# The order of the seven products of a weight pair, and where the seventh operand of the feed-forward is made

## The chip, the cores and the metric

One core of a Trainium2 chip runs the whole kernel. The metric is the device time of one execution in microseconds, as the median of several runs. The engines work side by side and are tied by semaphores: TensorE (PE) multiplies, VectorE (DVE) combines two tensors, ScalarE (ACT) copies, casts and applies functions, GpSimd (POOL) issues accumulating DMAs here, and SyncE (SP) issues all other DMAs.

## What is computed

One layer of a bidirectional encoder on 1024 positions of 1024 channels, in float32. The two parts that the change touches are dense projections: the combined input projection of the token mixers, and the gated feed-forward.

```
proj = h @ W_in                          # h: 1024 x 1024, W_in: 1024 x 8192
...
x  = x + y @ W_out
h2 = rmsnorm(x)
gate, val = split(h2 @ W_up)             # W_up: 1024 x 5632, D_FF = 2816
x  = x + (silu(dwconv3(gate)) * val) @ W_down
return rmsnorm(x)
```

## The kernel before

Activations lie transposed, with 128 channels on the partitions and 512 positions (a half) in a page of 128 x 512. Each float32 operand is split into a high part in a rounded format (fp32r) and the remainder as a low part (`split`, L120: ScalarE casts the high part, VectorE subtracts for the low part), and a product of two blocks is three matmuls, high-high, high-low and low-high (`mm3`, L138 to L145).

**Pairs.** 34 of the 64 column blocks of the input projection (17 pairs) and all 44 of the feed-forward's up projection (22 pairs: a gate block and the value block that belongs to it) are worked in pairs by a Strassen-like scheme of seven products instead of eight (`pair_job`, L223). A pair is a 2 x 2 matrix of quadrants (two halves of positions, two column blocks) over an inner dimension cut into two times four blocks of 128. A product is 4 blocks x 3 matmuls = 12 matmuls. Seven operands come from the activations, `acts(i)`, as differences and sums of the four quadrants b11, b12, b21, b22; seven from the weights, `w[i]`.

`prep` (L231 to L254) makes the weight operands: two raw tiles are loaded by SP (`raw_w` into tag `wr`; `sw`), a third (`w4`, the quadrant a22); GpSimd adds by accumulating DMAs (L237), and after each sum a cast and a subtraction split the result. Pages of tag `wp` hold operands 1 and 2, then 6 and 3 (4 buffers, in the main pool); pages of tag `wq` hold 7 and 5 together and 4 (3 buffers, in the pool `wpool`). The single `sw` tile is free for the next pair when 7 and 5 have been split.

`run` (L256 to L282) issues the products to TensorE in the order 1, 2, 6, 7, 5, 4, 3. Products 1, 6, 5 and 3 accumulate in one PSUM bank, `row` (tag `mm`, 3 buffers), 2 has a bank of its own (`tr`), 7 and 4 share `col` (`sc`). ScalarE copies a running sum out of a bank (`copy`, L265: p1 after 1, u2 after 6, p7 after 7), and VectorE makes the quadrants from such a copy and a bank (`evac`). TensorE's order is the order in which the program writes the matmuls, by hand; the other engines' orders and the DMA queues come from a planner that takes instructions as they become ready in its own estimate, the earlier written first. A write to a bank waits for the reads of it that were written before.

`run_jobs` (L149) prepares the weights of the next pair after four pieces (products 1 and 2) of the present one.

**The feed-forward's operands.** While the output projection `w_out` runs, each new page of normalised input (`x2`, scaled but without the row's norm factor) is stored to DRAM (`d_h2`) and kept in the pool `p4`. The loop at L1111 makes operands 1, 2, 6 and 5 from these tiles into 32 pages `hx` in the main pool. Then `p4` is released and the pool `fu` is laid over the same memory; a tile there waits until the tiles that lay under it are no longer used. Operands 7, 4 and 3 are made after the first products of the feed-forward have been issued, from reloads of `d_h2` (`late_load`, L1189; `late_parts`, L1186): eight loads for 7, four for 4, four for 3, through 4 pages `ft`.

**The gate.** `ffn_job` (L1131): quadrants with e = 0 are the gate columns, written to a padded row `gp` and scaled (L1142, L1144); quadrants with e = 1 are the values (L1138). When the second half of the gate has come, for both halves ScalarE and VectorE do the three taps (L1150, L1154), Silu (L1162), the norm factor (L1163), the product with the value (L1164) and the store to `d_g` (L1165). After the feed-forward the down projection reloads `d_g` in groups (`load_g`, L1220), and its first pass copies banks to `xr` (L1230).

Of the kernel before, what the change touches and what calls it, by code (L numbers as in the profile page):

```python
# [10 lines left out]
F32 = mybir.dt.float32  # L11
F32R = mybir.dt.float32r
# [3 lines left out]
ALU = mybir.AluOpType  # L16
AX = mybir.AxisListType

P = 128
# [25 lines left out]
def tile_hybrid_encoder(  # L45
# [22 lines left out]
    nc = tc.nc  # L68
    PSUM = bass.MemoryType.PSUM
    V, A, G, T = nc.vector, nc.scalar, nc.gpsimd, nc.tensor  # L70
# [20 lines left out]
    def nm(s):  # L91
        uid[0] += 1
        return f"{s}_{uid[0]}"
# [3 lines left out]
    def bank(tag):  # L97
        return ps.tile([P, H], F32, tag=tag, name=nm(tag), bufs=BANKS[tag])

    def page(pool, tag, bufs, dt=F32):  # L100
        return pool.tile([P, H], dt, tag=tag, name=nm(tag), bufs=bufs)

    def tmp():
        return page(mp, "tm", 4)
# [4 lines left out]
    def hx():  # L109
        return page(mp, "hx", 32, F32R)  # L110
# [6 lines left out]
    def split_lo(eng, lo, src, hi):  # L117
        eng.tensor_tensor(lo, src, hi.bitcast(F32), op=ALU.subtract)  # L118

    def split(hi, lo, src, eng):  # L120
        A.copy(hi, src)  # L121
        split_lo(eng, lo, src, hi)
        return hi, lo
# [4 lines left out]
    def raw_w(src, nk):  # L128
        t = mp.tile([P, nk, P], F32, tag="wr", name=nm("wr"), bufs=2)
        nc.sync.dma_start(t, src)  # L130
        return t

    def w_page(nk, pool=None):
        if pool is None:
            return mp.tile([P, nk, P], F32R, tag="wp", name=nm("wp"), bufs=4)
        return pool.tile([P, nk, P], F32R, tag="wq", name=nm("wq"), bufs=3)

    def mm3(acc, w, act, k, first, last, again=False):  # L138


        whi, wlo = w
        ahi, alo = act
        T.matmul(acc, whi[:, k, :], ahi, start=first, stop=False, skip_group_check=again)  # L143
        T.matmul(acc, whi[:, k, :], alo, start=False, stop=False, skip_group_check=again)  # L144
        T.matmul(acc, wlo[:, k, :], ahi, start=False, stop=last, skip_group_check=again)  # L145
# [77 lines left out]
    def pair_job(src0, src1, nk, acts, wpool, pool, evac, su=4):  # L223

        def prep():  # L231
            def both(src, alt):
                hi, lo = split(w_page(2 * nk, alt), w_page(2 * nk, alt), src, V)
                return [(hi[:, :nk], lo[:, :nk]), (hi[:, nk:], lo[:, nk:])]

            def add(o, a):
                G.dma_start(o, a, accum_op=ALU.add)  # L237

            w = {}
            rows = raw_w(src0, 2 * nk)  # L240
            col = wpool.tile([P, 2 * nk, P], F32, tag="sw", name=nm("sw"), bufs=1)
            nc.sync.dma_start(col[:, :nk], src0[:, :nk])
            nc.sync.dma_start(col[:, nk:], src1[:, :nk])
            a22 = wpool.tile([P, nk, P], F32, tag="w4", name=nm("w4"), bufs=1)
            nc.sync.dma_start(a22, src1[:, nk:])
            add(col, src1)
            w[1], w[2] = both(rows, None)
            add(rows[:, :nk], col[:, nk:])
            w[7], w[5] = both(col, wpool)
            add(rows[:, nk:], rows[:, :nk])  # L250
            w[6], w[3] = both(rows, None)
            one = w_page(2 * nk, wpool)
            w[4] = split(one[:, :nk], one[:, nk:], a22, V)
            return w  # L254

        def run(w):  # L256
            def product(i, acc, first=True):
                for k in range(nk):
                    mm3(acc, w[i], acts(i)[k], k, first and k == 0, k == nk - 1, not first)
                    if k % 2 == 1 or k == nk - 1:  # L260
                        yield

            def copy(acc):
                t = page(pool, "su", su)
                A.copy(t, acc)  # L265
                return t

            row, b2, col = bank("mm"), bank("tr"), bank("sc")
            yield from product(1, row)
            p1 = copy(row)  # L270
            yield from product(2, b2)
            evac(0, 0, b2, p1, ALU.add)
            yield from product(6, row, False)
            u2 = copy(row)
            yield from product(7, col)
            p7 = copy(col)
            yield from product(5, row, False)
            evac(1, 1, p7, row, ALU.subtract)
            yield from product(4, col, False)
            evac(1, 0, col, u2, ALU.subtract)  # L280
            yield from product(3, row, False)
            evac(0, 1, row)  # L282

        return prep, run

# [88 lines left out]
    def scratch(name, *dims):  # L374
        if not dims:
            return dp.tile([P, H], F32, name=name)
        return [scratch(f"{name}_{i}", *dims[1:]) for i in range(dims[0])]
# [14 lines left out]
    d_g = scratch("d_g", NF, 2)  # L392
# [5 lines left out]
    NK2 = ND // 2  # L398
# [128 lines left out]
    for k in range(NK2):  # L527
        b21 = page(p1, "su", 4)
# [133 lines left out]
    for half in range(2):  # L662
        xs = []
        for j in range(NCW):
            if j % 2 == 0:
                both = p1.tile([P, 2, H], F32, tag="ca", name=nm("cx"), bufs=2)
# [16 lines left out]
        for j, xn in enumerate(xs):  # L683
# [3 lines left out]
            both = gp0.tile([P, 2, H], F32R, tag="gl", name=nm("ch"), bufs=NCW)  # L687
# [313 lines left out]
    for h in range(NH):  # L1001
# [4 lines left out]
        for half in range(2):  # L1006
            i = 2 * h + half
# [33 lines left out]
    fw = tc.alloc_tile_pool(name="fw", bufs=1, reuse_waits="tile")  # L1041
# [30 lines left out]
    h2 = {i: [] for i in range(1, 8)}  # L1072
# [23 lines left out]
        return evac  # L1096

    h2_pages = {i: [(hx(), hx()) for _ in range(NK2)] for i in (1, 2, 6, 5)}

    def parts(i, k, src):  # L1100
        h2[i].append(split(*h2_pages[i][k], src, V))
# [9 lines left out]
    for k in range(NK2):  # L1111
        s_out.fill(16 if k else 17) if k < NK2 - 1 else s_out.drain()
        b11, b12, b21, b22 = x2[k][0], x2[k][1], x2[k + NK2][0], x2[k + NK2][1]
        t5, t6 = tmp(), tmp()
        parts(1, k, b11)
        V.tensor_tensor(t5, b11, b12, op=ALU.subtract)
        parts(2, k, b21)
        V.scalar_tensor_tensor(t6, t5, -1.0, b22, op0=ALU.mult, op1=ALU.subtract)
        parts(6, k, t6)
        parts(5, k, t5)  # L1120
    p4.release()


    fu = tc.alloc_tile_pool(name="fu", bufs=1, reuse_waits="tile")
# [5 lines left out]

    def ffn_job(j):  # L1131
        g = gp[j % 2]
        val = [None, None]

        def evac(e, half, x0, x1=None, op=None):
            if e == 1:
                val[half] = page(fu, "ft", 4)
                V.tensor_tensor(val[half], x0, x1, op=op)  # L1138
                return
            gh = g[:, 1 + half * H : 1 + (half + 1) * H]  # L1140
            if x1 is not None:
                V.tensor_tensor(gh, x0, x1, op=op)  # L1142
                x0 = gh
            V.tensor_tensor(gh, x0, rstd2[half], op=ALU.mult)  # L1144
            if half == 0:
                return
            for hf in range(2):
                o = hf * H
                c = tmp()
                A.activation(  # L1150
                    c, g[:, o : o + H], AF.Identity, scale=vec("fdw", j), bias=vec("fdb", j)
                )
                for k in (1, 2):
                    V.scalar_tensor_tensor(  # L1154
                        c,
                        g[:, o + k : o + k + H],
                        vec("fdw", k * NF + j),
                        c,
                        op0=ALU.mult,
                        op1=ALU.add,  # L1160
                    )
                A.activation(c, c, AF.Silu)  # L1162
                V.tensor_tensor(c, c, rstd2[hf], op=ALU.mult)  # L1163
                V.tensor_tensor(val[hf], val[hf], c, op=ALU.mult)  # L1164
                nc.sync.dma_start(d_g[j][hf], val[hf])  # L1165

        return pair_job(
            w_cols(ffn_w_up, 0, ND, j * P),
            w_cols(ffn_w_up, 0, ND, DFF + j * P),
            NK2,  # L1170
            lambda i: h2[i],
            fw,
            fu,
            evac,
            su=3,
        )
# [7 lines left out]
    rstd2 = [next(st) for st in stats]  # L1184

    def late_parts(i, src):  # L1186
        h2[i].append(split(page(fu, "hy", 24, F32R), page(fu, "hy", 24, F32R), src, V))

    def late_load(kk, half):  # L1189
        t = page(fu, "ft", 4)  # L1190
        nc.sync.dma_start(t, d_h2[kk][half])
        return t

    for k in range(NK2):
        b12, b22 = late_load(k, 1), late_load(k + NK2, 1)
        V.tensor_tensor(b12, b12, b22, op=ALU.subtract)
        late_parts(7, b12)
    for k in range(NK2):
        b21 = late_load(k + NK2, 0)
        for part in h2[6][k]:  # L1200
            V.tensor_tensor(b21, b21, part.bitcast(F32), op=ALU.add)
        late_parts(4, b21)
    for k in range(NK2):
        late_parts(3, late_load(k + NK2, 1))
    s_ffn.drain()
    fu.release()
    fw.release()
# [149 lines left out]
```

## Time and profile before

| | us |
|---|---|
| median of 3 runs | 1918.57 |
| lowest and highest | 1916.76 and 1922.56 |
| the profiled execution | 1916.23 |
| its span, first to last instruction | 1914.5 |
| mean granted TensorE clock | 0.974 |

How to read the profile: the page gives for each engine its busy time; a row of the view by stretch gives for a window, in microseconds from the span's start, the busy time and number of instructions of each engine (PE, PEld for the loading of weights, DVE, ACT, POOL), then the granted clock of TensorE, the share of the DMA engines and their rate. A row in order of time reads: start, duration, engine, line, operation, out<-in by names, shapes, count, and in brackets the idle time of the engine just before and what ended it. The shown duration of a matmul is longer than the distance to the next one, since they are pipelined; the distance between two starts is what counts. DMA rows (SPq, and L237 on POOL) show the issue, not the transfer. A row of the list of waits has: who waited for whom, microseconds in total, times, longest. A row of the DMA issues ends with the size and the median microseconds from issue to landing.

### The profile page before, as it was taken

To read this page: it belongs to the slowest core of one execution; us is meant where nothing else is said; L and a number is where in the kernel's file an instruction comes from. 1 tells how busy PE (TensorE), PEld (TensorE's weight loads), DVE (VectorE), ACT (ScalarE), POOL (GpSimd) and SP (SyncE) were. 2 spreads that over 40 slices of the span, in tenths; PEclk is the share of its full clock that TensorE was granted. 3 is DMA by queue.
4 is the path that set the end of the run, shared out by engine and by line. 5 is a ranking of instruction groups with operands and counts; after the bars stand their busy time and mean duration, and the time that the engine had idled before them with its cause. 6 is when DMAs were issued, how large, how long until landed. Compare 5 with 4: busy or idle time off the path is not lost.

```text
span 1914.5 us, 23761 instructions
## 1 busy us (share of the span) xinstructions
PE 1805.9 (94%) x8543; PEld 1484.6 (78%) x8543; DVE 1271.6 (66%) x1860; ACT 799.3 (42%) x1488; POOL 217.9 (11%) x218
## 2 busy tenths in 40 slices
PE   6989999999989999998997999899999999999996
PEld 4767888877778787887875888588888888788885
DVE  3488999535479898898845655766666666634445
ACT  6334343334555565455343134544443444522124
POOL 3101112213000101101000000111111111000000
PEclk8999999999999999999997999899999999999998
DMA  7747788885652332332227666767767775733134
GB/s 254 218 123 166 177 197 194 198 176 133 212 173 83 107 125 93 112 111 73 71 89 232 202 189 184 193 148 160 148 149 148 151 152 124 220 93 98 54 90 160
DMA packets 324492, 286.14 MB, mean 149 GB/s; under 512 B 14990, under 2 KB 245142, under 8 KB 324374
## 3 DMA queue, kind: packets, MB, share of 16 engines
q1 hardware_dynamic: 272582, 243.72, 41.1%
q0 software_dynamic: 51792, 40.90, 15.2%
q8 instruction: 67, 1.10, 0.2%
q14 instruction: 51, 0.42, 0.1%
HBM read 191.76 MB, written 72.35 MB: 138 GB/s over the span
## 4 chain that ended last, share of the span: by engine, by line
PE 60%; DVE 15%; DMA 11%; ACT 6%; issue 4%; POOL 2%; SPq 0%; ACTq 0%; POOLq 0%; DVEq 0%
PE mm L143 15%; PE mm L144 15%; PE mm L145 15%; PE sc L144 3%; PE sc L145 3%; PE sc L143 3%; DVE wp L118 2%; DVE acc L644 2%; DMA sw<-in_ffn_w_up_dram 2%; DMA sw<-in_w_in_dram 1%; DMA wr<-wr 1%; PE tr L145 1%; PE tr L143 1%; PE tr L144 1%; DVE DE L729 1%
## 5 line engine op out<-in xcount | busy, mean ns | idle before, releaser
L143 PE MATMUL mm<-hx,wp 128*128 128x512 f32 x1176 | 482.2, 410 | 21.6 <-ACT hx L121 6.3
L145 PE MATMUL mm<-hx,wp 128*128 128x512 f32 x1176 | 467.8, 398 | 3.7 <-DVE wp L118 3.7
L144 PE MATMUL mm<-hx,wp 128*128 128x512 f32 x1176 | 467.1, 397 | 3.3 <-POOL hx L118 1.9
L121 ACT CAST wp<-wr 128x1024 fp32r<-128x1024 f32 (+2 forms) x196 | 179.8, 918 | 337.2 <-PE mm L144 207.8
L118 DVE TENSOR_TENSOR wp<-wr,wp 128x1024 fp32r<-128x1024 f32 (+2 forms) x196 | 207.1, 1057 | 116.9 <-ACT wp L121 110.5
L143 PEld LDWEIGHTS mm<-hx,wp 128*128 128x128 f32 x1176 | 226.1, 192 | 72.0 <-ACT hx L121 8.5
L145 PEld LDWEIGHTS mm<-hx,wp 128*128 128x128 f32 x1176 | 225.2, 191 | 55.6 <-DVE wp L118 6.3
L144 PEld LDWEIGHTS mm<-hx,wp 128*128 128x128 f32 x1176 | 226.1, 192 | 49.9 <-POOL hx L118 3.5
L644 DVE SCALAR_TENSOR_TENSOR acc<-gl,v_b,acc 128x1024 f32<-128x1024 f32 x120 | 149.2, 1278 | 0.5
L143 PE MATMUL sc<-hy,wq 128*128 128x512 f32 x244 | 97.1, 398 | 2.8 <-ACT hy L121 2.8
L144 PE MATMUL sc<-hy,wq 128*128 128x512 f32 x244 | 96.7, 396 | 2.9 <-DVE hy L118 2.9
L145 PE MATMUL sc<-hy,wq 128*128 128x512 f32 x244 | 96.3, 395 | 0.0
L237 POOL DMA_DIRECT2D wr<-sw x39 | 34.9, 896 | 510.5 <-DVE wp L118 272.8
L1236 DVE TENSOR_TENSOR xr<-mm,xr 128x512 f32<-128x512 f32 x48 | 33.1, 690 | 81.5 <-PE mm L145 81.5
L837 PEld LDWEIGHTS sc<-qF,A 128*128 128x128 f32 x512 | 65.9, 193 | 19.2 <-ACT A L834 8.0
L837 PE MATMUL sc<-qF,A 128*128 128x128 f32 x512 | 69.2, 279 | 11.7 <-DVE qF L729 6.1
L121 ACT CAST wq<-sw 128x1024 fp32r<-128x1024 f32 x39 | 41.1, 1053 | 85.3 <-PE mm L144 66.6
L143 PE MATMUL mm<-hy,wp 128*128 128x512 f32 x156 | 63.2, 405 | 8.5 <-ACT wp L121 5.8
L1154 DVE SCALAR_TENSOR_TENSOR tm<-gp,v_a,tm 128x512 f32<-128x512 f32 x88 | 65.7, 747 | 1.8 <-ACT tm L1150 0.9
L265 ACT COPY su<-mm 128x512 f32<-128x512 f32 x78 | 45.3, 581 | 47.9 <-PE mm L145 47.9
L834 ACT COPY A<-kG 128x512 f32<-128x512 f32 x64 | 39.6, 619 | 58.1 <-DVE kG L729 42.7
L403 POOL TENSOR_SCALAR ors<-oss 128x4 f32<-128x4 f32 x16 | 13.8, 865 | 439.0 <-ACT jk L947 439.0
(281 smaller groups left out, 3564.5 us busy)
## 6 DMA issues: line engine op xcount, KB each, us to landing
wr<-in_w_in_dram SPq DMA_DIRECT2D x55, 512.0 KB, 5.8
sw<-in_ffn_w_up_dram SPq DMA_DIRECT2D x44, 256.0 KB, 3.3
sw<-in_ffn_w_up_dram POOLq DMA_DIRECT2D x22, 512.0 KB, 8.2
wr<-in_ffn_w_up_dram SPq DMA_DIRECT2D x22, 512.0 KB
d_g<-ft SPq DMA_DIRECT2D x44, 256.0 KB, 5.3
ev<-d_g SPq DMA_DIRECT2D x44, 256.0 KB, 3.1
wr<-sw POOLq DMA_DIRECT2D x39, 256.0 KB, 3.3
wr<-wr POOLq DMA_DIRECT2D x39, 256.0 KB, 4.4
```

The costliest lines, as they stand in the source:

```text
L118: eng.tensor_tensor(lo, src, hi.bitcast(F32), op=ALU.subtract)
L121: A.copy(hi, src)
L143: T.matmul(acc, whi[:, k, :], ahi, start=first, stop=False, skip_group_check=again)
L144: T.matmul(acc, whi[:, k, :], alo, start=False, stop=False, skip_group_check=again)
L145: T.matmul(acc, wlo[:, k, :], ahi, start=False, stop=last, skip_group_check=again)
L237: G.dma_start(o, a, accum_op=ALU.add)
L265: A.copy(t, acc)
L644: V.scalar_tensor_tensor(acc, g[:, k : k + S], tap(k), acc, op0=ALU.mult, op1=ALU.add)
L834: A.copy(A_t.rearrange("p (b x e) -> p b x e", x=2, e=h), pairs(kG, h))
L837: T.matmul(b[:, c * P : (c + 1) * P].rearrange("p (b x e) -> p b x e", x=2, e=h), A_t[:, c * P : (c + 1) * P], view(qF, c * P, [[2 * h, P ...
L1154: V.scalar_tensor_tensor(c, g[:, o + k : o + k + H], vec("fdw", k * NF + j), c, op0=ALU.mult, op1=ALU.add,)
L1236: V.tensor_tensor(xr[i][half], acc, xr[i][half], op=ALU.add)
```

## The change

The order of the products becomes 1, 2, 6, 5, 7, 3, 4, for the pairs of both stages. The copy p7 goes, a copy u5 of `row` after product 5 comes. In the feed-forward, operand 7 is made in the loop of the output projection from tiles on the chip, as t7 = b12 - b22, into 16 pages of its own (tag `h7`, pool `fw`), and operand 6 comes from t7; the reloads for 7 go, and operand 3 is made before 4. The weight pages `w4` and `wq` of the pair move from the pool `wpool` to `pool`: nothing moves in the input projection, where both are the same pool; in the feed-forward they go from `fw` to `fu`. The gate of a pair is now complete after product 3, before the value of the first half; `join` multiplies and stores the second half then, and the first half after product 4.

```diff
@@ pair_job, prep
-            a22 = wpool.tile([P, nk, P], F32, tag="w4", name=nm("w4"), bufs=1)
+            a22 = pool.tile([P, nk, P], F32, tag="w4", name=nm("w4"), bufs=1)
...
-            w[7], w[5] = both(col, wpool)
+            w[7], w[5] = both(col, pool)
...
-            one = w_page(2 * nk, wpool)
+            one = w_page(2 * nk, pool)
@@ pair_job, run
             yield from product(6, row, False)
             u2 = copy(row)
+            yield from product(5, row, False)
+            u5 = copy(row)
             yield from product(7, col)
-            p7 = copy(col)
-            yield from product(5, row, False)
-            evac(1, 1, p7, row, ALU.subtract)
+            evac(1, 1, col, u5, ALU.subtract)
+            yield from product(3, row, False)
+            evac(0, 1, row)
             yield from product(4, col, False)
             evac(1, 0, col, u2, ALU.subtract)
-            yield from product(3, row, False)
-            evac(0, 1, row)
@@ operands of the feed-forward
+    h2_pages[7] = [[page(fw, "h7", 2 * NK2, F32R) for _ in range(2)] for _ in range(NK2)]
...
-        t5, t6 = tmp(), tmp()
+        t7, t6, t5 = tmp(), tmp(), tmp()
         parts(1, k, b11)
+        V.tensor_tensor(t7, b12, b22, op=ALU.subtract)
+        parts(2, k, b21)
+        V.tensor_tensor(t6, t7, b11, op=ALU.subtract)
+        parts(6, k, t6)
         V.tensor_tensor(t5, b11, b12, op=ALU.subtract)
-        parts(2, k, b21)
-        V.scalar_tensor_tensor(t6, t5, -1.0, b22, op0=ALU.mult, op1=ALU.subtract)
-        parts(6, k, t6)
         parts(5, k, t5)
+        parts(7, k, t7)
@@ ffn_job
+        def join(hf):
+            V.tensor_tensor(val[hf], val[hf], gate[hf], op=ALU.mult)
+            nc.sync.dma_start(d_g[j][hf], val[hf])
...
                 V.tensor_tensor(val[half], x0, x1, op=op)
+                if half == 0:
+                    join(0)
...
-                c = tmp()
+                c = gate[hf] = tmp()
...
-                V.tensor_tensor(val[hf], val[hf], c, op=ALU.mult)
-                nc.sync.dma_start(d_g[j][hf], val[hf])
+            join(1)
@@ late operands
-        h2[i].append(split(page(fu, "hy", 24, F32R), page(fu, "hy", 24, F32R), src, V))
+        h2[i].append(split(page(fu, "hy", 16, F32R), page(fu, "hy", 16, F32R), src, V))
...
     for k in range(NK2):
-        b12, b22 = late_load(k, 1), late_load(k + NK2, 1)
-        V.tensor_tensor(b12, b12, b22, op=ALU.subtract)
-        late_parts(7, b12)
+        late_parts(3, late_load(k + NK2, 1))
...
-    for k in range(NK2):
-        late_parts(3, late_load(k + NK2, 1))
```

More of the change, by code (lines that the diff above doesn't have):

```diff
@@ L1132, in ffn_job @@
         g = gp[j % 2]
-        val = [None, None]
+        val, gate = [None, None], [None, None]
+        def join(hf):
+            V.tensor_tensor(val[hf], val[hf], gate[hf], op=ALU.mult)
+            nc.sync.dma_start(d_g[j][hf], val[hf])
         def evac(e, half, x0, x1=None, op=None):
```

## The prediction

> **What bounds the kernel now.** I read the first page for the engines, then the busy time by stretch for the two stages that multiply by pairs of weight columns (17 pairs of the input projection, about 120 to 480 us; 22 of the feed-forward, 1199 to 1645 us), then single engines in order of time around one pair.
>
> ```profile
> span 1914.5 us, 23761 instructions
> ...
> PE 1805.9 (94%) x8543; PEld 1484.6 (78%) x8543; DVE 1271.6 (66%) x1860; ACT 799.3 (42%) x1488; POOL 217.9 (11%) x218
> ```
>
> ```profile
> core 0: us, PE busy (x) PEld busy (x) DVE busy (x) ACT busy (x) POOL busy (x), PEclk, DMA share, GB/s
> 1207.50:1235.40 27.90, 20.97 (x58) 12.93 (x57) 20.32 (x31) 12.04 (x20) 1.82 (x2) 0.76 0.63 186
> 1649.90:1659.00 9.10, 4.44 (x13) 3.16 (x13) 4.33 (x8) 4.55 (x8) 0.00 (x0) 0.81 0.87 281
> 120.00:480.00 360.00, 349.20 (x1507) 283.61 (x1506) 272.74 (x287) 130.47 (x187) 73.88 (x66) 0.99 0.74 171
> 1245.00:1640.00 395.00, 394.51 (x1720) 321.97 (x1719) 262.60 (x353) 165.49 (x231) 65.09 (x59) 1.00 0.69 149
> 600.00:700.00 100.00, 94.71 (x602) 82.55 (x601) 91.04 (x168) 56.74 (x132) 7.92 (x8) 1.00 0.36 111
> 1400.00:1500.00 100.00, 100.00 (x438) 81.60 (x437) 64.42 (x86) 40.66 (x56) 17.58 (x16) 1.00 0.69 147
> ```
>
> TensorE sets the pace. From 1400 to 1500 us it does 438 matmuls without a hole, 0.228 us each; so a product (12 matmuls) is 2.74 us and a pair (84) 19.2 us. Against that rate 1245 to 1640 us loses 395 - 1720 x 0.228 = 2.3 us, and 120 to 480 us loses 360 - 1507 x 0.228 = 15.9 us. Two short stretches are bad: 27.9 - 58 x 0.228 = 14.7 us at the head of the feed-forward and 9.1 - 13 x 0.228 = 6.1 us at the start of the down projection. A wait put into TensorE's order inside the pairs therefore costs its full length, and what the change can win near its edits is the 14.7 and the 6.1 us.
>
> **The change part by part: the new order, 39 times.** Products 1, 6, 5 and 3 accumulate in one PSUM bank (row); ScalarE copies running sums out of it. Before, each copy had another product to hide behind: that of 1 behind 2, that of 6 behind 7. After, 5 follows 6 in the same bank, so its first matmul waits until the copy u2 has read it. Today's end of product 6 and its copy, then a place where a matmul already waits for such a copy:
>
> ```profile
> 346.78 0.39 PE L145 MATMUL mm<-hy,wp 128*128 128x512 f32 x1
> ```
>
> ```profile
> 347.20 0.59 ACT L265 COPY su<-mm 128x512 f32<-128x512 f32 x1 [1.89 <-PE mm L145]
> ```
>
> ```profile
> 402.76 0.59 ACT L265 COPY su<-mm 128x512 f32<-128x512 f32 x1
> ```
>
> ```profile
> 403.40 0.50 PE L143 MATMUL mm<-hy,wp 128*128 128x512 f32 x1 [1.38 <-ACT su L265]
> 403.74 0.40 PE L144 MATMUL mm<-hy,wp 128*128 128x512 f32 x1
> 403.97 0.39 PE L145 MATMUL mm<-hy,wp 128*128 128x512 f32 x1
> ```
>
> A free ScalarE starts the copy 0.42 us after the start of the product's last matmul (346.78 to 347.20) and takes 0.59; TensorE starts 0.05 after its end (403.35 to 403.40), and the first step after the wait is 0.34 instead of 0.23. From that last matmul to the second of product 5: 0.42 + 0.59 + 0.05 + 0.34 = 1.40 us, where two steps take 0.46 today: **0.94 us a pair, 39 pairs, 36.7 us.** Less is excluded: the steps are serial, and nothing else stands in TensorE's order between 6 and 5. Behind the waiting matmul are products 5, 7, 3, 4 and the next pair; the combinations on VectorE and the copies on ScalarE wait for those, so the whole pair moves.
>
> On top comes what stands before u2 on ScalarE. In the input projection that is nothing (1.89 us idle ahead of 347.20). In the feed-forward, after a product 6 whose last matmul started at 1302.23:
>
> ```profile
> 1302.23 0.39 PE L145 MATMUL mm<-hx,wp 128*128 128x512 f32 x1
> ```
>
> ```profile
> 1302.83 0.82 ACT L1150 ACTIVATE tm<-gp,v_c,v_a 128x512 f32<-128x512 f32 x1 [0.42 <-DVE gp L1144]
> 1303.56 0.56 ACT L265 COPY su<-mm 128x512 f32<-128x512 f32 x1
> ```
>
> The gate's first activation goes ahead, and the copy starts 1.33 us after the last matmul, 0.91 more. Bounds: 0 and 22 x 0.91 = 20 us. With product 3 now sixth, the previous pair's gate work starts a product earlier, so VectorE and ScalarE should reach this activation sooner; I take the end nearer to 0, 0.2 us a pair, **4.4 us**.
>
> The other exchanges cost nothing. u5 replaces p7, one copy each, and has product 7 (2.74 us) as cover before 3 needs the bank. The subtraction that frees the bank of 7 and 4 has product 3 as cover, as it had 4 before. Without cover each would be one more wait of about 1 us a pair.
>
> **The head of the feed-forward.** Product 7's operand came from reloads; now 8 of the 16 remain, for 3 and 4, and those come last.
>
> ```profile
> 1201.25 27.71 SPq L1191 DMA_DIRECT2D ft<-d_h  x15
> ```
>
> ```profile
> 1209.79 0.69 DVE L1196 TENSOR_TENSOR ft<-ft,ft 128x512 f32<-128x512 f32 x1 [3.42 <-DMA ft<-d_h]
> ```
>
> ```profile
> 1211.18 0.50 PE L143 MATMUL sc<-hy,wq 128*128 128x512 f32 x1 [0.33 <-ACT hy L121]
> 1212.87 0.50 PE L144 MATMUL sc<-hy,wq 128*128 128x512 f32 x1 [1.19 <-DVE hy L118]
> ...
> 1223.17 0.63 PE L145 MATMUL mm<-hx,wq 128*128 128x512 f32 x1
> 1223.60 0.63 PE L143 MATMUL mm<-hx,wq 128*128 128x512 f32 x1
> ```
>
> Product 7 starts at 1211.18 and crawls behind the reloads, and the clock falls (steps of 0.43). After, 5 and 7 run there without reloads; 3 starts at about 1211.2 + 1 + 2 x 2.74 = 1217.7, when its four tiles (the first came at 1209.8) can be split: four casts and four subtractions of 0.7 us. Operand 4 needs its loads into pages that 3 frees, then twelve VectorE steps of 0.69 us (8.3 us), from about 1214.5 to 1223, against a start of product 4 at 1220.5: 2 to 3 us remain late.
>
> Four more splits and four subtractions move into the loop of the output projection (ScalarE 4 x 0.62, VectorE 8 x 0.69 = 5.5 us). TensorE works there for w_out, and after its last product VectorE still has the hole of 3.42 us above; cost 0. Without that cover it is the last quarter, 1.4 us.
>
> Against this stands the move of the weight pages of 5, 7 and 4 and of the raw a22 into the second pool, which lies on tiles of the output projection. The first pair's column weights were fetched as early as 1011 us and cast at once, so the raw tile was free for pair two at 1193:
>
> ```profile
> 1011.54 1.63 POOL L237 DMA_DIRECT2D sw<-in_ffn_w_up_dram  x1 [4.39 <-DVE hx L118]
> ...
> 1199.19 1.57 POOL L237 DMA_DIRECT2D sw<-in_ffn_w_up_dram  x1 [4.94 <-DMA sw<-in_ffn_w_up_dram]
> ...
> 1212.51 0.95 POOL L237 DMA_DIRECT2D wr<-sw  x1 [7.58 <-DVE wp L118]
> 1217.51 0.87 POOL L237 DMA_DIRECT2D wr<-wr  x1 [4.04 <-DMA wr<-sw]
> ```
>
> ```profile
> 1193.17 0.38 SPq L242 DMA_DIRECT2D sw<-in_ffn_w_up_dram  x1
> ```
>
> ```profile
> sw<-in_ffn_w_up_dram POOLq DMA_DIRECT2D x22, 512.0 KB, 8.2
> ...
> wr<-wr POOLq DMA_DIRECT2D x39, 256.0 KB, 4.4
> ```
>
> ```profile
> 1211.00 1.22 DVE L118 TENSOR_TENSOR wp<-wr,wp 128x1024 fp32r<-128x1024 f32 x1
> ```
>
> Now that cast waits for the last w_out matmul (about 1199), so pair two's loads go behind 1205, its accumulating DMA (8.2 us to land) from 1199 to about 1210, and the two that follow on the same queue by 5 us or so, to land near 1227 instead of 1222 (1217.5 + 4.4); product 6 of pair two starts near 1229 and needs a cast and a subtraction (1.22 alone) first. So 1 us may be late there. Of the 14.7 us I take **11 won**; bounds 14.7 won and 5 lost (the chain of pair two as late as it can be against today's hiding).
>
> **The start of the down projection.** Its first copies queue on ScalarE behind casts that wait for reloads, which share the SP queue with the last pair's stores:
>
> ```profile
> 1653.86 0.62 ACT L121 CAST hx<-ev 128x512 fp32r<-128x512 f32 x1 [1.07 <-DMA ev<-d_g]
> 1654.38 1.55 ACT L1230 COPY xr<-mm 128x512 f32<-128x512 f32 x3
> ```
>
> One of the two stores now leaves with product 3 and only a product and a store hang on 4, so the reloads can go sooner; the order of the queues can also come out otherwise. Bounds 6.1 won, 3 lost; I take **1.5 won**.
>
> **Sum.** Against the profiled execution's own 1916.2 us: 36.7 + 4.4 - 11 - 1.5 = +28.6, so 1944.8. The median of the runs shown is 2.3 us above that execution (1918.57, from 1916.76 to 1922.56), so **1947 us**.
>
> **The rivals.** (a) *The copy stays queued* behind the activation as in the rows of 1302.83 and 1303.56, in every feed-forward pair: 20 instead of 4.4, 1963 us. For it: that order is fixed today; against: the gate work moves forward. (b) *The head wins nothing*: the first pair's weights wait for the released tiles, or the reloads for 3 and 4 are issued as late as those for 7 were: 11 us more, 1958. This is also the case in which the change doesn't do what it says. (c) *The waits are swallowed*, the other side: pairs could be paced by the weight chain (SP load, three accumulating DMAs, cast), TensorE only filling the time, so a hole before 5 shortens a later one. Then the 36.7 falls to near 0 and the time is 1918.6 - 12.5 = 1906; it decides from 12.5 / 39 = 0.32 us a pair downwards. For it: DMA share 0.69 to 0.74 in both stages; against it, plainly: TensorE has 2.3 us of holes in the 395 us there. (d) *The clock falls at each wait.* In the stretch with the 4.66 us hole (clock 0.81 over 9.1 us) about 0.38 x 9.1 = 3.5 us went at half speed, 1.7 us lost; 39 times that is 68 us, 2015 us. Against it: the hole of 1.38 us at 403.40 is followed by steps of 0.34 and 0.23, full rate, and 600 to 700 us, with 5.3 us of holes, shows clock 1.00. The Trainium skill (TensorE: Matmul & The Clock Gate, "A second HAM failure mode: psum-queue depth-cycling") says that short idling between groups of matmuls at each change of PSUM bank can make the clock swing between half and full; the section before it puts the limit at gaps above some 3.4 us. By the first the change would cost (d), by the second nothing; the row of 403.40 agrees with the second, so I keep (d) small.
>
> **How the numbers follow.** Forecast 0.66, (a) 0.16, (b) 0.11, (c) 0.04, (d) 0.03. The forecast's own bounds, with the copies at 0 to 10 us, the head at 7 to 14.7 won and the tail as above, run from 1934 to 1963. Range 1934 to 1966: it takes in (a) and (b), and leaves out (c), (d) and the corners. A measurement of this kernel tells about 0.3%, 6 us, from no change; only (c) is faster (0.04), the rest of the corners gives 0.02 for within that, and slower has 0.94.
>
> **What would show it.** The list of waits has this row:
>
> ```profile
> PE mm L143 <- ACT su L265: 2.0, 4, 1.4
> ```
>
> In the changed profile: before the first matmul of product 5 an idle time of 0.6 to 1.4 us, put down to the copy on ScalarE, 39 times, some 30 us where that row has 2.0; in 1245 to 1640 us, 0.94 us or more lost per pair at clock 1.00; in the head, product 7 without waits for reloads and 3 to 5 us lost in all. It is wrong if product 5 starts 0.23 us after 6 ends its issue, if the pairs' period stays at 19.2 us, or if the clock shows half speed between pairs.

## The result and the profile after

| | before | after |
|---|---|---|
| median, us (lowest to highest, runs) | 1918.57 (1915.14 to 1922.56, 5) | 1943.65 (1941.32 to 1948.62, 5) |
| ratio after/before, 95% interval | | 1.0135 (1.0117 to 1.0153) |
| profiled execution, us (its span) | 1916.2 (1914.5) | 1947.76 (1946.0) |

The change costs 25.1 us between the medians, where 28.6 were forecast. The two profiled executions lie 31.5 us apart. First the engines on the page of the changed kernel:

```profile
PE 1810.5 (93%) x8543; PEld 1479.4 (76%) x8543; DVE 1267.2 (65%) x1860; ACT 802.3 (41%) x1488; POOL 218.6 (11%) x218
```

TensorE has the same 8543 matmuls and 4.6 us more of busy time; the rest of the 31.5 us is time in which it stood still. The busy time by stretch, in the stage of the feed-forward's pairs:

```profile
core 0: us, PE busy (x) PEld busy (x) DVE busy (x) ACT busy (x) POOL busy (x), PEclk, DMA share, GB/s
1245.00:1660.00 415.00, 397.66 (x1707) 319.01 (x1708) 264.06 (x355) 169.11 (x230) 66.64 (x60) 1.00 0.65 142
...
1400.00:1500.00 100.00, 95.73 (x413) 76.70 (x412) 61.77 (x83) 39.07 (x55) 16.65 (x15) 1.00 0.64 141
```

In the hundred microseconds that held 438 matmuls there are 413 now, at the same clock of 1.00. Over the long stretch 415 - 1707 x 100/438 = 25.3 us are lost, where 2.3 were lost in the 395 us that the prediction read. TensorE's list of waits (total us, times, longest) says to what:

```profile
PE mm L143 <- ACT su L265: 31.1, 41, 1.1
...
PE sc L143 <- DVE ev L587: 7.3, 3, 5.1
...
PE mm L143 <- ACT xr L1234: 3.2, 1, 3.2
...
PE sc L411 <- DVE gp L1151: 2.9, 1, 2.9
```

The first row is the forecast one: the copy on ScalarE out of the bank "row", 41 times and 31.1 us in place of 4 times and 2.0; 39 of the 41, with 29.3 us, stand before the first matmul of product 5. One such place, TensorE from the last matmul of product 6 to the second of product 5 (start, us, then the operation; in brackets the idle time before it), and ScalarE beside it:

```profile
1339.55 0.39 PE L145 MATMUL mm<-hx,wp 128*128 128x512 f32 x1
1340.67 0.50 PE L143 MATMUL mm<-hx,wq 128*128 128x512 f32 x1 [0.73 <-ACT su L265]
1341.01 0.39 PE L144 MATMUL mm<-hx,wq 128*128 128x512 f32 x1
```

```profile
1338.79 0.82 ACT L1159 ACTIVATE tm<-gp,v_c,v_a 128x512 f32<-128x512 f32 x1 [0.66 <-DVE gp L1153]
1340.03 0.58 ACT L265 COPY su<-mm 128x512 f32<-128x512 f32 x1 [0.43 <-PE mm L145]
```

The gate's activation that stood in front of the copy at 1302.83 before is done 0.4 us before the copy is wanted. The copy starts 0.48 us after the last matmul, takes 0.58, TensorE follows 0.06 later and its first step is 0.34: from 1339.55 to 1341.01 1.46 us, where two steps took 0.46, so 1.00 us a pair. Read in this way at all 39 places, the loss is 0.95 us at 14 of the 17 pairs of the input projection, 1.00 at 18 of the 22 of the feed-forward, never under 0.95 nor over 1.36, and 40.0 in all.

Here is where TensorE reaches the same point of the work, in the two profiled executions:

| first matmul of | before | after | shift |
|---|---|---|---|
| product 2 of the projection's first pair | 139.31 | 141.26 | +1.95 |
| product 2 of its 5th pair | 225.60 | 231.67 | +6.07 |
| product 2 of its 10th pair | 322.53 | 333.44 | +10.91 |
| product 2 of its 11th pair | 341.57 | 361.49 | +19.92 |
| product 2 of its 17th pair | 463.96 | 486.31 | +22.35 |
| the mixers' output projection | 1009.03 | 1032.39 | +23.36 |
| the feed-forward | 1198.12 | 1218.09 | +19.97 |
| product 2 of its second pair | 1239.26 | 1253.27 | +14.01 |
| product 2 of its 22nd pair | 1625.50 | 1659.33 | +33.83 |
| the down projection, behind its copies | 1655.01 | 1688.66 | +33.65 |
| the last transposes | 1901.34 | 1932.87 | +31.53 |

The feed-forward grows by 19.8 us over the 20 pairs between its two rows, 0.99 each. The input projection grows by 20.4 over 16 pairs; 16 x 0.95 is 15, and most of the rest comes in one step, at the 11th pair:

```profile
348.86 0.39 PE L145 MATMUL mm<-hx,wp 128*128 128x512 f32 x1
354.33 0.69 PE L143 MATMUL sc<-hx,wq 128*128 128x512 f32 x1 [5.09 <-DVE ev L587]
354.82 0.63 PE L144 MATMUL sc<-hx,wq 128*128 128x512 f32 x1
```

VectorE in that time:

```profile
344.66 7.88 DVE L644 SCALAR_TENSOR_TENSOR acc<-gl,v_b,acc 128x1024 f32<-128x1024 f32 x6
352.46 1.22 DVE L118 TENSOR_TENSOR wq<-sw,wq 128x1024 fp32r<-128x1024 f32 x1
353.60 0.68 DVE L587 TENSOR_TENSOR ev<-sc,su 128x512 f32<-128x512 f32 x1
```

Product 4 waits for the subtraction that empties its bank. The cover was product 3, 2.74 us; but on VectorE six accumulations of 1.3 us and the split of a weight page stood in front of it.

### The profile page after: what moved, and what is told of

It is laid out like the page before. It is cut to its first block, busy times and chain, and to the rows that moved or that the text cites. A ratio compares the mean times of both kernels' runs of the same rounds, so it can differ in the third digit from the quotient of the medians.

```text
span 1946.0 us, 23732 instructions
## 1 busy us (share of the span) xinstructions
PE 1810.5 (93%) x8543; PEld 1479.4 (76%) x8543; DVE 1267.2 (65%) x1860; ACT 802.3 (41%) x1488; POOL 218.6 (11%) x218
## 4 chain that ended last, share of the span: by engine, by line
PE 61%; DVE 14%; DMA 10%; ACT 7%; issue 4%; POOL 2%; SPq 0%; ACTq 0%; POOLq 0%; DVEq 0%
PE mm L143 15%; PE mm L144 15%; PE mm L145 15%; PE sc L143 3%; PE sc L144 3%; PE sc L145 3%; DMA sw<-in_w_in_dram 2%; DVE wp L118 2%; DMA wr<-wr 1%; DVE acc L644 1%; PE sc L837 1%; PE tr L145 1%; PE tr L143 1%; PE tr L144 1%; DVE DE L729 1%
## 5 line engine op out<-in xcount | busy, mean ns | idle before, releaser
L265 ACT COPY su<-mm 128x512 f32<-128x512 f32 x117 | 68.0, 582 | 157.6 <-PE mm L145 157.5
L1145 DVE TENSOR_TENSOR ft<-sc,su 128x512 f32<-128x512 f32 x44 | 30.2, 686 | 119.8 <-issue 115.3
L143 PE MATMUL mm<-hy,wp 128*128 128x512 f32 x156 | 62.5, 401 | 5.4 <-ACT wp L121 3.5
L143 PE MATMUL sc<-hy,wq 128*128 128x512 f32 x156 | 62.0, 397 | 2.0 <-DVE ft L1145 1.8
L145 PE MATMUL mm<-hy,wp 128*128 128x512 f32 x156 | 62.1, 398 | 0.0
```

## The experiments

**The old order in the changed kernel.** Products, copies, the gate's joining and the order of the late operands as before; the seventh operand from tiles on the chip and the weight pages in their new pool stay.

```diff
-            yield from product(5, row, False)
-            u5 = copy(row)
             yield from product(7, col)
-            evac(1, 1, col, u5, ALU.subtract)
-            yield from product(3, row, False)
-            evac(0, 1, row)
+            p7 = copy(col)
+            yield from product(5, row, False)
+            evac(1, 1, p7, row, ALU.subtract)
             yield from product(4, col, False)
             evac(1, 0, col, u2, ALU.subtract)
+            yield from product(3, row, False)
+            evac(0, 1, row)
...
-                if half == 0:
-                    join(0)
...
-    for k in range(NK2):
-        late_parts(3, late_load(k + NK2, 1))
...
+    for k in range(NK2):
+        late_parts(3, late_load(k + NK2, 1))
```

> The changed kernel with the products in the order of before (1, 2, 6, 7, 5, 4, 3, the copy p7, the gate finished last, operand 4 made before 3); operand 7 is still made from tiles on the chip and the weight pages still lie in the second pool. Theory (the wait between 6 and 5 is the whole loss, about 0.95 us a pair plus some 4 us of other waits in the pairs; the head is a gain of 7 us): 1943.7 - 39 x 0.95 - 4 = about 1903 to 1911 us, faster than the kernel before. Rival (the moved weight pages or the work moved into the output projection's loop cost time, and the head is no gain by itself): 1920 us or more. In the list of waits the row of the first matmul of a bank waiting for the copy falls from 31.1 us to about 2.

Measured: 1906.63 us (1901.56 to 1910.94, 6 runs) against 1918.02 of before, ratio 0.9937 (0.9920 to 0.9954), and 37.0 below the changed kernel. This version beats both kernels, the one before by 0.6%. Few waits for copies are left in its list, 4.7 us where about 2 were expected:

```profile
PE mm L143 <- ACT su L265: 4.7, 4, 2.2
```

Its head shows the step that the forecast named as next in line, the weight chain of the second pair. TensorE comes to product 2 of that pair 30.6 us after the first product (1196.67 to 1227.31) instead of 41.1, and then waits, because ScalarE's copy of p1 stands behind a cast whose weights have not landed:

```profile
1228.13 1.05 ACT L121 CAST wp<-wr 128x1024 fp32r<-128x1024 f32 x1 [5.32 <-DMA wr<-wr]
...
1231.74 0.57 ACT L265 COPY su<-mm 128x512 f32<-128x512 f32 x1
```

```profile
1232.37 0.50 PE L143 MATMUL mm<-hx,wp 128*128 128x512 f32 x1 [2.17 <-ACT su L265]
...
1233.92 0.63 PE L143 MATMUL mm<-hx,wp 128*128 128x512 f32 x1
```

Of 10.5 us won, 4 go back here: 6.4 us are left at the third pair. The wait of 2.17 us is also most of what the row of the copies has beyond the 2.0 of before.

**The order alone in the kernel before.** The same edit the other way round: new order, joined gate, late operands in the order 7, 3, 4; operand 7 still from reloads, weight pages where they were.

```diff
-            yield from product(7, col)
-            p7 = copy(col)
             yield from product(5, row, False)
-            evac(1, 1, p7, row, ALU.subtract)
-            yield from product(4, col, False)
-            evac(1, 0, col, u2, ALU.subtract)
+            u5 = copy(row)
+            yield from product(7, col)
+            evac(1, 1, col, u5, ALU.subtract)
             yield from product(3, row, False)
             evac(0, 1, row)
+            yield from product(4, col, False)
+            evac(1, 0, col, u2, ALU.subtract)
...
```

> The kernel before with nothing but the new order (1, 2, 6, 5, 7, 3, 4, the copy u5, and the gate joined in two steps, as that order needs); operand 7 comes from reloads and the weight pages lie where they lay; the late operands are made in the order 7, 3, 4. Theory: 39 waits of 0.95 us and the failing covers in the input projection, without the gain at the head: 1918.6 + 37 + 3 = 1955 to 1963 us, 8 to 15 us slower than the changed kernel. Rival (the head of the changed kernel gained nothing): 1943 to 1947 us, the same as the changed kernel.

Measured: 1959.64 us (1956.83 to 1960.75, 4), ratio 1.0212 (1.0195 to 1.0228). Its list of waits:

```profile
PE mm L143 <- ACT su L265: 31.1, 40, 1.8
...
PE mm L143 <- ACT hx L121: 10.5, 2, 9.3
...
PE sc L143 <- ACT hy L121: 9.0, 3, 7.4
```

The first row is again 31.1, so the waits belong to the order and not to the other parts. The second lies mostly at 1040 to 1049 us, in the mixers' output projection, and is a cost of its own beside them. It is part of why this kernel is 16.0 us slower than the changed one, where 8 to 15 were expected:

```profile
1047.63 1.04 ACT L121 CAST wq<-sw 128x1024 fp32r<-128x1024 f32 x1 [9.28 <-DMA sw<-in_ffn_w_up_dram]
```

A cast of the feed-forward's first weights, whose pages are free this early, holds up ScalarE for 9.28 us until its loads land, with the casts of the reloaded mixer outputs queued behind it; the mixers' output projection takes TensorE 105.8 us here up to `w_out` and 101.9 before, 3.9 of the 6.3 us by which its shift against before grows from the input projection's last pair to the feed-forward (19.75 to 26.03). The third row is the head, where the 7.4 us are product 4 waiting for its operand, the last of three that come from reloads here: 3.6 us more than before up to the second pair. So the order without the seventh operand's new source costs more than both together.

**The copy twice.** In the changed kernel u2 is copied a second time into the same tile; product 5 has to wait for both.

```diff
             u2 = copy(row)
+            A.copy(u2, row)
```

> The changed kernel with the copy u2 written twice by ScalarE, one after the other into the same page. Theory (TensorE waits for the copy itself, link by link): 0.56 us more in each of 39 pairs, 22 us, about 1965 us, and a wait of 1.2 to 1.3 us instead of 0.68 to 0.73. Rival (the wait is a fixed price of writing to the bank that was just finished, or of the semaphore, with the copy beside it): no more than 5 us more, 1944 to 1949 us.

Measured: 1960.96 us (1956.41 to 1968.53, 4), ratio 1.0234 (1.0209 to 1.0259), 17.3 more than the changed kernel.

```profile
PE mm L143 <- ACT su L275: 54.6, 39, 2.1
```

```profile
1363.51 0.39 PE L145 MATMUL mm<-hx,wp 128*128 128x512 f32 x1
...
1365.25 0.50 PE L143 MATMUL mm<-hx,wq 128*128 128x512 f32 x1 [1.35 <-ACT su L275]
```

Locally the copy is paid in full: 1.74 us from the end of 6 to the start of 5 where 1.12 stood, 0.62 each and 39 times, and the 39 waits grow by (54.6 - 29.3) / 39 = 0.65 on average. So the pairs are not paced by the weight chain, which would have hidden part of it. The medians have 17.3 of these 24.2 us, and the two profiled executions lie only 8.6 apart in their spans (1954.6 and 1946.0). Between those two, the usual pair of the feed-forward shows the copy in full (20.89 us against 20.27). The projection's 11th pair gives 7.4 us back (20.6 us here, from 334.73 to 355.36, against 28.1), because the subtractions ahead of product 4 cost 2.5 us of waits and not 7.3. Another 7.4 us are won ahead of the projection's first pair and behind the last pair of the feed-forward, where the edit changes nothing. So the price is shown where it arises; why the medians keep only 17.3 of it is not settled.

**The new order in the feed-forward alone.** A branch on the number of the copies' pages gives the input projection its old order (and its copy of product 7).

```diff
+            if su == 4:
+                yield from product(6, row, False)
+                u2 = copy(row)
+                yield from product(7, col)
+                p7 = copy(col)
...
+                return
```

> The changed kernel with the order of before in the 17 pairs of the input projection, and the new order in the 22 of the feed-forward only. Theory: 17 waits of 0.94 us and the 5 us lost to other waits in that stage go: 1943.7 - 16 - 5 = 1920 to 1928 us. Rival (the stage of the scan behind it takes back what the projection loses, as the profile of the changed kernel shows 4 us of it): 1926 to 1932 us.

Measured: 1926.55 us (1923.79 to 1929.56, 5), ratio 1.0042 (1.0028 to 1.0057), 17.1 less than the changed kernel with 17 pairs put back, 1.0 us for each.

```profile
PE mm L143 <- ACT su L265: 18.3, 23, 1.1
```

The price goes by the number of pairs that have the new order, in either stage. The time alone lies in the ranges of both the theory and the rival. The profile decides against the rival, by which the stage of the scan takes back what the projection wins: TensorE reaches product 2 of the projection's last pair 19.6 us sooner than in the changed kernel (466.70 against 486.31), and that of the feed-forward's first pair 24.1 us sooner (1198.44 against 1222.51).

**The weight pages alone.** In the kernel before, the pages of 5, 7, 4 and of the raw a22 go to the second pool; nothing else is changed.

```diff
-            a22 = wpool.tile([P, nk, P], F32, tag="w4", name=nm("w4"), bufs=1)
+            a22 = pool.tile([P, nk, P], F32, tag="w4", name=nm("w4"), bufs=1)
...
-            w[7], w[5] = both(col, wpool)
+            w[7], w[5] = both(col, pool)
...
-            one = w_page(2 * nk, wpool)
+            one = w_page(2 * nk, pool)
```

> The kernel before with nothing but the move of the weight pages of products 7, 5 and 4 and of a22 from the first pool of the feed-forward to the second. Theory: the move has two effects of opposite sign. Ahead of the output projections the first pair's cast of these weights no longer stands in ScalarE's queue, where it waited 5 us for its DMA with the casts of the mixer's reloads behind it: about 3.5 us won by the first matmul of w_out. At the head of the feed-forward the cast now stands before the scalings for the norm factor, and product 7 comes fourth: 3 to 6 us lost. Sum 1916 to 1922 us, the same as before. Rival (the move only costs, as the prediction had it): nothing won before w_out and 1920 to 1926 us.

Measured: 1916.95 us (1908.06 to 1919.32, 11), ratio 0.9989 (0.9971 to 1.0006): no difference that the interval shows, and made of two effects. The pages lie on tiles of the output projections, so the early cast cannot stand in ScalarE's queue there any more. Before, it did:

```profile
1021.72 1.04 ACT L121 CAST wq<-sw 128x1024 fp32r<-128x1024 f32 x1 [5.30 <-DMA tm<-d_bm]
1022.67 2.17 ACT L121 CAST hx<-tm 128x512 fp32r<-128x512 f32 x4
```

```profile
1023.34 0.79 PE L143 MATMUL mm<-hx,wp 128*128 128x512 f32 x1 [4.48 <-ACT hx L121]
```

Without it the longest wait there is 1.8 us, and TensorE is 3.6 us sooner through this place. On the other side the head takes longer with the pages moved: 42.29 us from the first product (1190.97) to the second pair's product 2 (1233.26), 1.15 more than before, where 3 to 6 were expected. The two leave a gain of 2.4 us, which lies inside the interval (5.6 us faster to 1.2 slower).

**The factors spread on VectorE.** From the first experiment's kernel; the eight scalings of the identity by the norm's factors, which come late on ScalarE in the head, are made on VectorE.

```diff
+            if eng is not None:
+                eng.tensor_scalar(diag[:, c * P : (c + 1) * P], ident, r[:, c : c + 1], None, op0=ALU.mult)
+                continue
...
-    stats = [rstd_over_partitions(sq, D, "sc", sq) for sq in sq_sum]
+    stats = [rstd_over_partitions(sq, D, "sc", sq, V) for sq in sq_sum]
```

> The kernel e1_old_order with the eight scalings of the identity that spread the feed-forward's norm factor done by VectorE, not by ScalarE. Theory (the wait of 2.9 us before the first spreading matmul, and the half clock after it, come from the moved weight casts ahead of these scalings on ScalarE): the wait falls below 1 us and 2 to 4 us are won: 1902 to 1905 us. Rival (the wait comes from something else: GpSimd's power, the bank, VectorE, which the list of waits names): the wait stays at 2 to 3 us, 1905 to 1910 us.

Measured: 1909.43 us (1906.24 to 1912.46, 6), ratio 0.9945 (0.9924 to 0.9966): no gain over the 0.9937 without it.

```profile
1208.62 1.10 PE L414 MATMUL sc<-tm,ones_m 128*128 128x512 f32 x2 [1.56 <-DVE tm L411]
1210.28 1.10 PE L414 MATMUL sc<-tm,ones_m 128*128 128x512 f32 x2 [0.56 <-DVE tm L411]
...
1225.94 0.65 PE L143 MATMUL mm<-hy,wp 128*128 128x512 f32 x1 [3.45 <-DVE ft L1144]
```

The place itself improves, from 6.05 us between the end of product 2 and the start of 6 to 4.14, though the wait before the first spreading matmul did not fall below the expected 1 us. But the next wait grows to 3.45 us. It is for the subtraction L1144 that empties the bank of product 3, on VectorE:

```profile
1223.37 1.23 DVE L118 TENSOR_TENSOR wq<-sw,wq 128x1024 fp32r<-128x1024 f32 x1 [1.72 <-ACT wq L121]
...
1225.12 0.68 DVE L1144 TENSOR_TENSOR ft<-su,mm 128x512 f32<-128x512 f32 x1
```

The subtraction stands behind the split of the next pair's weight page, for which VectorE waits until ScalarE has cast it; in the first experiment's kernel it ran ahead of that split.

**Another order, with the wait elsewhere.** In the changed kernel the order 1, 7, 6, 2, 5, 3, 4: u2 is covered by product 2, and the copy u5 is what product 3 waits for.

```diff
-            yield from product(2, b2)
-            evac(0, 0, b2, p1, ALU.add)
+            yield from product(7, col)
             yield from product(6, row, False)
             u2 = copy(row)
+            yield from product(2, b2)
+            evac(0, 0, b2, p1, ALU.add)
             yield from product(5, row, False)
             u5 = copy(row)
-            yield from product(7, col)
             evac(1, 1, col, u5, ALU.subtract)
```

> The changed kernel with the products in the order 1, 7, 6, 2, 5, 3, 4: product 2 now covers the copy u2, and 3 follows 5 in the same bank with the copy u5 between them. Theory (the price belongs to two products that follow each other in one bank with a copy between, whichever they are): the wait of 0.68 to 0.73 us stands before product 3 instead of 5, 39 times again, and the time is that of the changed kernel, 1940 to 1952 us, the upper part if product 7, now second, waits for the first pair's weights at the head. Rival (it is something of the pair 6 and 5, such as the change of weight pages from wp to wq): the waits go and 1905 to 1915 us is left.

Measured: 1991.7 us (1987.73 to 1993.99, 4), ratio 1.0372 (1.0346 to 1.0398). The wait moved as expected, but its size was missed by a factor of two and more:

```profile
PE mm L143 <- ACT su L265: 76.1, 45, 5.6
```

```profile
1381.76 1.04 ACT L121 CAST wq<-sw 128x1024 fp32r<-128x1024 f32 x1 [0.22 <-PE mm L144]
1382.71 0.58 ACT L265 COPY su<-mm 128x512 f32<-128x512 f32 x1
```

```profile
233.47 0.79 PE L143 MATMUL mm<-hx,wp 128*128 128x512 f32 x1 [5.65 <-ACT su L265]
234.06 0.63 PE L144 MATMUL mm<-hx,wp 128*128 128x512 f32 x1
...
1383.35 0.50 PE L143 MATMUL mm<-hy,wp 128*128 128x512 f32 x1 [1.39 <-ACT su L265]
```

The end of product 5 also frees the pages of the column weights, and the next pair's cast (1.04 us) goes in front of the copy: 1.39 us of wait in place of 0.73. In the input projection, where such casts themselves wait for loads, it is up to 5.65, followed by steps at half the rate (234.06 to 234.49). That is the queue that rival (a) described, and where the wait is long the fall of the clock of (d), at another place of the pair.

Weight pages in their old pool together with the new pages of operand 7 were not tried.

## Why the prediction held, and where its sizes did not

**The waits, 36.7 us forecast.** Shown. The row is there 41 times, is 1.00 us a pair in the feed-forward, and grows by a copy's length when the copy is doubled; the changed kernel and the first experiment, which differ in the order and what hangs on it, are 37.0 us apart; putting 17 pairs back returns 17.1. With the usual loss of a pair in the projection and the growth of a pair in the table for the feed-forward it is 17 x 0.95 + 22 x 0.99 = 37.9.

**ScalarE's queue, 4.4 us forecast.** Sized too high: the activation comes early enough, as 1338.79 shows, and the whole surplus of the feed-forward is 0.05 a pair, 1.1 us, which the 37.9 already hold. This settles rival (a) for this order: its 20 us do not come.

**The other exchanges, 0 forecast.** In the profiled execution this failed by 7.3 us, at three places where product 3 was too short a cover for the subtraction, and the half rate behind 354.33 came on top. It is not a property of the new order alone, nor equally large each time: such waits for VectorE's subtractions in the input projection, for another bank in the old order, come to 1.0 us in the kernel before and 3.1 and 3.8 in the first and fourth experiment (old order there), and with the new order to 5.3 us in the second experiment and 2.5 with the copy twice. My step read the cover's length and not what stands ahead of the subtraction on VectorE.

**The head, 11 us forecast.** 6.9: product 2 of the second pair comes 35.18 us after the first product where 41.14 stood, and 1 us of that is the head's own new wait. So 7.8 of the 14.7 us stayed lost, where 3 to 5 were named as the sign of a right forecast. Product 4 came out about as forecast, with 1.8 us of wait for its bank and 1.2 for its operand where 2 to 3 were to remain. Of the 4 us missing, 3.7 stand at one place that the forecast did not read: from the last matmul of product 2 to the first of product 6, where the matmuls that spread the norm's factors stand, 2.34 us before and 6.05 after. TensorE there before, in the changed kernel, and in the fifth experiment, which moves the weight pages alone:

```profile
1205.79 2.29 PE L411 MATMUL sc<-tm,ones_m 128*128 128x512 f32 x4 [0.23 <-ACT tm L410]
```

```profile
1225.15 0.39 PE L145 MATMUL tr<-hx,wp 128*128 128x512 f32 x1
1228.41 3.60 PE L411 MATMUL sc<-tm,ones_m 128*128 128x512 f32 x4 [2.87 <-DVE gp L1151]
```

```profile
1200.12 2.30 PE L411 MATMUL sc<-tm,ones_m 128*128 128x512 f32 x4 [1.69 <-ACT tm L410]
```

They wait for the scalings L410 on ScalarE. (For the changed kernel the list names VectorE, whose gp had come last by the profile; the scalings run until 1229.) ScalarE in the changed kernel:

```profile
1224.91 1.04 ACT L121 CAST wq<-sw 128x1024 fp32r<-128x1024 f32 x1
...
1226.37 0.57 ACT L265 COPY su<-mm 128x512 f32<-128x512 f32 x1
1226.85 0.69 ACT L410 ACTIVATE tm<-ident,r 128x128 f32<-128x128 f32 x2
1227.44 0.60 ACT L121 CAST wq<-w 128x512 fp32r<-128x512 f32 x1
```

The two weight casts, 1.64 us, go in front of the scalings. In the fifth experiment they do so too, and the place takes 3.81 us, so 1.5 of the 3.7 us come from the moved pages. The forecast had put these at 1 us, in the weight chain of the second pair. The other 2.2 us appear only in the kernels that also make operand 7 on the chip: 6.05 us in the changed kernel and in the first, third and fourth experiment, against 2.34 in the second. This points to the extra work in the loop of the output projection, which the forecast put at 0, or 1.4 without cover; no run has that work alone. In these kernels the first scaling starts 6.00 us after the first product instead of 5.34, one more cast of an operand stands among the scalings, and the four spreading matmuls take 2.79 us up to product 6 instead of 1.73, 0.85 to 1.01 us from start to start where 0.54 to 0.63 stood. The sixth experiment took half of the place's cost away and got nothing for the total, since VectorE was late next; so I can say where the missing 4 us stood, not that they were to be had.

**The weight pages elsewhere.** I had counted only a cost. They also won 3.4 us at the reloads of the mixer outputs (from +23.36 to +19.97 in the table); the fifth experiment, with the pages alone, shows 3.6.

**The start of the down projection, 1.5 us forecast.** The idle time fell from 4.66 to 3.17 us, 1.5. That it hit so closely is luck: this wait is 4.7 to 5.8 us in the four profiles with the old order in the feed-forward, and 3.2, 2.1, 0.2 and 1.9 in the changed kernel, the second, third and fourth experiment. The direction holds in all of them, and the size does not.

**The remaining rivals.** (b) fell: the head won 6.9. (c) fell with the doubled copy. (d) fell: the stretch of 1245 to 1660 us with its 20 waits has clock 1.00. The Trainium skill (TensorE: Matmul & The Clock Gate, "A second HAM failure mode: psum-queue depth-cycling") would have put the clock at half and full by turns there; with idle times of 0.73 us between the groups the trace shows none of it.

**What stays open.** The terms as measured, 37.9 for the waits, less 6.9, 3.4 and 1.5, make 26.1, against 25.1 between the medians. So the time came within 3.4 us of the forecast partly by luck: the queue on ScalarE, forecast some 3.3 too high, and the gain that was not counted stand against the 4.1 missing at the head. The sum leaves out the failing covers. The two profiled executions are 6.4 us further apart than the medians, and these covers (7.3 after, 1.0 before) are as large as that, but from one execution of each I cannot say how often they fail, nor does the median show that they fail less; this was not settled. The bounds that the prediction names for its terms add up to 1961 us at the top, not to its 1963; the measured time lies far from either.

## What to carry to other kernels

Between two accumulations in one PSUM bank with a copy between them, the price here was the copy's whole round trip, and it could be read from a place where the trace already had one; look for an order in which another bank's product stands there. Before a cover is called sufficient, add up what is queued in front of the covered instruction on its own engine, at its worst place and not its mean one. Moving buffers between pools moves the moment at which loads and casts enter an engine's queue: look at both ends, where they leave and where they arrive.

## What the runs showed of the chip that was not expected

An idle time near 2.4 us before a matmul was followed by half rate or by full rate. The same wait near the end of the kernel, on TensorE before the change, with the busy time by stretch behind it (columns as above, the clock third from the end):

```profile
1889.26 0.50 PE L143 MATMUL mm<-hx,wp 128*128 128x512 f32 x1 [2.37 <-ACT wp L121]
```

```profile
1888.00:1895.00 7.00, 5.74 (x19) 4.27 (x20) 3.47 (x6) 2.77 (x11) 0.00 (x0) 0.76 0.31 101
```

and after it:

```profile
1922.38 0.50 PE L143 MATMUL mm<-hx,wp 128*128 128x512 f32 x1 [2.48 <-ACT wp L121]
```

```profile
1921.00:1928.00 7.00, 5.62 (x25) 4.37 (x26) 4.47 (x7) 3.70 (x18) 0.00 (x0) 1.00 0.35 108
```

The shorter one is followed by a clock of 0.76 over 7 us, 0.24 x 7 = 1.7 us of work lost, the longer by full rate; that is most of the 2.1 us by which the shift shrinks from the down projection's start to the end. In the nine profiles of this document the wait at this place is 2.37 to 2.48 us; three of them (before, 2.43 us in the fourth experiment and 2.48 in the seventh) have steps of 0.43 us behind it, six only of 0.23 to 0.39. Elsewhere in the other runs 1.39 us was followed by full rate, 2.17 by half rate after 1.5 us, and 5.09 and 5.65 by half rate at once. The Trainium skill (TensorE: Matmul & The Clock Gate, "HAM oscillation — how this bites in real kernels") puts the limit at gaps of more than some 3.4 us; these rows put it lower here, so that 2.2 us can be enough and 2.5 need not be.
